# Two-layer decoder trunk on one core: when VectorE forms four sums, splits one small weight, and where seven-product pairs stand in one output product

## The chip, the cores and the metric

The kernel runs on one core of one Trainium2 chip. Its time is the device time in microseconds of the whole program; lower is better. Before the change the median of three runs is 2401.25 us (2401.14, 2401.25 and 2406.06).

## The reference

A trunk of two layers for 256 tokens of width 2048, all in float32. Layer 0 mixes tokens by retention, layer 1 by multi-head latent attention (MLA); each mixer is followed by a SwiGLU. Every sub-layer is `x + post_norm(f(pre_norm(x)))`. What the change touches:

```python
def mla(x, ...):
    c = x @ w_in                                   # latents c_q, c_kv (512 each) and k_r (64)
    c_q, c_kv, k_r = jnp.split(c, [MLA_Q_LORA, MLA_Q_LORA + MLA_KV_LORA], axis=-1)
    ...
    k_rope = rope(k_r[:, :, None, :], positions)   # the rotary key
    ...
    return o @ w_out                               # o: 256 x 2048, w_out: 2048 x 2048

def swiglu(x, w_gu, w_down):                       # in both layers
    gate, up = jnp.split(x @ w_gu, [D_FF], axis=-1)
    return (jax.nn.silu(gate) * up) @ w_down       # D_FF 5632
```

## The kernel before

Each float32 operand is split into a high part (a cast on ScalarE, L210) and a low part (source minus high part, a subtraction on VectorE, L211), and each product is three products on TensorE: high by high, high by low, low by high. SyncE's queue streams the weights as tiles of 128x1024 into four raw buffers; five pairs of slots hold their high and low parts. Matrix products run in the order retention, gu0_0 to gu0_10 (the gate and up product of layer 0, in groups of 1024 columns), dn0 (down), mc (MLA's latents), the rotary key, query products with attention, mlo (MLA's output product, two halves of 1024 columns), gu1_0 to gu1_10, dn1. A group has four PSUM banks: b00 and b01 for the first 128 tokens (t=0), b10 and b11 for the other 128 (t=1), 512 columns each.

Some pairs of weight pieces (two neighbouring tiles of 128 rows) are done as a 2x2 block product with seven products in place of eight. This needs sums of weight blocks and sums of activation blocks, and afterwards sums of the products.

In gu groups 1 to 10 the first four pairs (pieces 0 to 7) are done so, by `first_sevens` (L425). Its tiles are named for what they hold: `b` and `a` are weight blocks and sums t1 to t3, `c` is the second raw tile of a pair, `d` holds t4. TensorE takes the b and a parts of all pairs first, then the c parts on b00 and b01, then the d parts on b10, then pieces 8 to 15 (`w8`, `w9`, ...). `fourth(p)` forms t4 of pair p on VectorE (L473) and splits it at once (`dhi` on ScalarE, `dlo` on VectorE). Between them VectorE also combines banks: L485, L488, L492, L495.

In mlo the function `closing` calls `group` for each half with `sevens` from `MLO_SEVENS`. Pairs of the list take their weight sums (L260 to L263), are split into `ta` and `tb` parts, and run 21 products; behind the last pair of a half, `combine` (L350 to L355) and four `adds` (L360) bring the sums into b00 to b11. In half 0 the pieces behind the last pair are run as they come; in half 1 the t=1 products of the last pieces, and the t=0 products of pieces 14 and 15, are held to the end. The activation sums of a pair are made once, by `left_sums` (L246 to L249), and shared by both halves.

In mc the normed input comes in pieces: TensorE transposes (`htp`, L602), VectorE scales (`hx`, L608), both split it (`hT`). The rotary key's weight `kr_raw` (128x16x64) is split into `kr_w`, used in 16 products (L1100) after mc.

The order on each engine is set by a scheduler from its own costs at build time, unless an instruction goes through `tc.keep_in_program_order`. `later(k, fn)` puts off a call by k weight loads (`step`). On the chip each engine takes its instructions in that fixed order.

Of the kernel before, what the change touches and what calls it, by code (L numbers as in the profile page):

```python
# [8 lines left out]
F32 = mybir.dt.float32  # L9
# [9 lines left out]
DT = D // P  # L19
# [15 lines left out]
GU_SEVENS = 4  # L35
DN_SEVENS = (2, 5, 7, 10, 12, 15, 17), (2, 4, 5, 7, 10, 12, 15, 17)
RTO_SEVENS = (3, 6, 9, 12), (3, 5, 6, 9, 12)
MLO_SEVENS = (3, 5), (1, 3)
QK_SEVENS, VG_SEVENS = (0, 2, 3, 3), 3

C_INV, C_ID, C_MASK, C_TWICE = 0, NF, NF + P, NF + 3 * P
# [17 lines left out]
def trunk(  # L59
# [19 lines left out]
    nc = tc.nc  # L79
# [8 lines left out]
    def misc_bank(name):  # L88
        return ps.tile([P, 512], F32, tag="misc", bufs=2, name=name)
# [43 lines left out]
    def later(k, fn):  # L133
        order[0] += 1
        todo.append((steps[0] + k, order[0], fn))
# [66 lines left out]
    def share(slots, room):  # L202

        both = 2 if slots >= 6 else 1 if slots >= 3 else 0
        return min(2, slots - 2 * both), both, room

    def split(hi, lo, src, g=None):

        if g is None:
            nc.scalar.copy(out=hi, in_=src)  # L210
            nc.vector.tensor_sub(out=lo, in0=src, in1=hi.bitcast(F32))  # L211
        else:
            nc.scalar.activation(out=hi, in_=src, func=AF.Copy, scale=g)
            nc.vector.scalar_tensor_tensor(
                out=lo, in0=src, scalar=g, in1=hi.bitcast(F32), op0=ALU.mult, op1=ALU.subtract
            )

    def weights(load, parts, name, raw_room=None, room=None):


        if raw_room is None:
            raw = wp.tile([P, 1024], F32, tag="raw", bufs=RAW, name=f"{name}_raw")
        else:
            raw = raw_room(F32, f"{name}_xraw")
        load(raw)
        if room is None:
            hi = wp.tile([P, 1024], F32R, tag="whi", bufs=WB, name=f"{name}_hi")
            lo = wp.tile([P, 1024], F32R, tag="wlo", bufs=WB, name=f"{name}_lo")
        else:
            hi, lo = room(F32R, f"{name}_xhi"), room(F32R, f"{name}_xlo")  # L230
        for a, n, g in parts:
            split(hi[:, a : a + n], lo[:, a : a + n], raw[:, a : a + n], g)
        return hi, lo, raw
# [10 lines left out]
    def left_sums(a00, a01, a10, a11, sums, hi, lo):  # L244

        nc.vector.tensor_sub(out=sums[:, 0], in0=a10, in1=a11)  # L246
        nc.vector.tensor_sub(out=sums[:, 1], in0=sums[:, 0], in1=a00)
        nc.vector.tensor_sub(out=sums[:, 2], in0=a00, in1=a10)
        nc.vector.tensor_add(out=sums[:, 3], in0=sums[:, 1], in1=a01)  # L249
        split(hi, lo, sums)  # L250
# [171 lines left out]
                )  # L422
                begun.add(bank)

    def first_sevens(lhs, kts, w, g, name, n, left, spare):  # L425

# [4 lines left out]
        raw1, t2, wt, last = {}, {}, {}, {}  # L433
# [5 lines left out]
        def parts(nm):  # L439
            hi = wp.tile([P, 1024], F32R, tag="whi", bufs=WB, name=f"{name}_{nm}hi")  # L440
            lo = wp.tile([P, 1024], F32R, tag="wlo", bufs=WB, name=f"{name}_{nm}lo")
            return hi, lo

        def half(x, i):
            return tuple(y[:, i * 512 : (i + 1) * 512] for y in x)
# [24 lines left out]
        def fourth(p):  # L470
            if p % 2 == 0:
                last[0] = parts("d")
            nc.vector.tensor_add(out=t2[p], in0=t2[p], in1=raw1[p][:, 0:512])  # L473
            wt["d", p] = half(last[0], p % 2)
            split(*wt["d", p], t2[p])

# [66 lines left out]
    def tile_load(w, g, name, halves=0, spare=(0, 0, None)):  # L543

        def load(kt, first_half=False):
            n = 512 if kt < halves or first_half else 1024  # L550

            def dma(raw):
                for a in range(0, 1024, 512 if kt < halves else 1024):
                    m = 512 if kt < halves else 1024
                    nc.sync.dma_start(out=raw[:, a : a + m], in_=w[g, kt, :, a : a + m])

            parts = [(a, n, None) for a in range(0, 512 if first_half else 1024, n)]
            raws, both, room = spare
            return weights(
                dma, parts, f"{name}_w{kt}", room if DT - 2 - raws <= kt < DT - 2 else None,  # L560
                room if kt >= DT - both else None,
            )

        return load
# [199 lines left out]
    def retention():  # L764
# [34 lines left out]
        def qk_group(gq, spare):  # L799
            name = f"rqk{gq}"  # L800
            if gq:
                return first_sevens(h_lhs, DT, ret_qk, gq, name, QK_SEVENS[gq], lambda p: ins[p], spare)
            return group(h_lhs, DT, tile_load(ret_qk, gq, name, 1, spare), name, lead=3)
# [167 lines left out]
    def swiglu(i):  # L971
        with tc.tile_pool(name=f"ff{i}", bufs=1) as fp:

            groups = FF // 512
            aT = {}

            def spare_a(kind, name):
                return fp.tile([P, 1024], kind, tag="aT", bufs=groups, name=name)

            def take_a(k0, n):  # L980
                return aT[k0 // 4][:, k0 % 4 : k0 % 4 + n]

            def transposes(j, t, a):
                if t == 0:
                    aT[j] = fp.tile([P, 4, NT, P], F32, tag="aT", bufs=groups, name=f"aT{i}{j}")
                tp = misc_bank(f"ftp{i}{j}{t}")
                for b in range(4):
                    nc.tensor.transpose(tp[:, b * P : (b + 1) * P], a[:, b * P : (b + 1) * P], ident)  # L988
                nc.scalar.copy(
                    out=aT[j][:, :, t, :], in_=tp.rearrange("p (j q) -> p j q", j=4)  # L990
                )

            def sums(n):
                f = wp.tile([P, 4, P], F32, tag="mv", bufs=MV, name=f"sf{i}")
                if n < 2:
                    hi = fp.tile([P, 4, P], F32R, tag="sa", bufs=4, name=f"sh{i}")
                    lo = fp.tile([P, 4, P], F32R, tag="sa", bufs=4, name=f"sl{i}")
                else:
                    hi = wp.tile([P, 4, P], F32R, tag="ah", bufs=3, name=f"sh{i}")
                    lo = wp.tile([P, 4, P], F32R, tag="al", bufs=3, name=f"sl{i}")  # L1000
                return f, hi, lo

            ins, where = gu_next[0]
            where[0] = sums

            for j in range(groups):
                name = f"gu{i}_{j}"
                spare = share(groups - j, spare_a)
                if j:
                    banks = first_sevens(  # L1010
                        h_lhs, DT, w_gu[i], j, name, GU_SEVENS, lambda p: ins[p], spare
                    )
                else:
                    banks = group(h_lhs, DT, tile_load(w_gu[i], j, name, 0, spare), name, lead=4)
                watch[0] = None
                both = fp.tile([P, NT, 512], F32, tag="fa", bufs=1, name="fa")
                for t in range(NT):
                    sg = fp.tile([P, 512], F32, tag="fsg", bufs=2, name="fsg")
                    nc.scalar.activation(out=sg, in_=banks[t][0], func=AF.Silu, scale=rx_next[t])
                    a = both[:, t, :]  # L1020
                    nc.vector.scalar_tensor_tensor(
                        out=a, in0=banks[t][1], scalar=rx_next[t], in1=sg, op0=ALU.mult, op1=ALU.mult
                    )
                    later(4 + t, lambda j=j, t=t, a=a: transposes(j, t, a))
            closing(
                take_a, FF // P, w_down[i], g_ffn_post[i],
                None if i else G_MIX + DT, f"dn{i}",
                lambda name: fp.tile([P, 1024], F32, tag="fa", bufs=1, name=name), sevens=DN_SEVENS,
            )


    def mla():
        with tc.tile_pool(name="ml", bufs=1) as mp:
# [18 lines left out]
            with tc.tile_pool(name="ml_c", bufs=1) as cp:  # L1052


                kr_raw = cp.tile([P, DT, ROPE], F32, name="kr_raw")
                kr_w = cp.tile([P, DT, 2, ROPE], F32R, name="kr_w")
                krp = cp.tile([P, 2, NT, P], F32, name="krp")

                def kr_weights():
                    nc.sync.dma_start(out=kr_raw, in_=mla_kr)  # L1060
                    for kt in range(DT):
                        split(
                            kr_w[:, kt, 0, :], kr_w[:, kt, 1, :], kr_raw[:, kt, :]
                        )

                later(10, kr_weights)
                cs = {}

                def kept(banks, t):
# [116 lines left out]
            with tc.tile_pool(name="ml_a", bufs=1) as ap:  # L1186
# [110 lines left out]
                for hp in range(AH // 2):  # L1297
# [5 lines left out]
                    lambda k0, n: oT[:, k0 : k0 + n], AH, mla_out, g_mix_post[1], G_FFN + DT, "mlo",  # L1303
                    lambda name: ap.tile([P, 1024], F32, tag="aqkT", bufs=1, name=name), sevens=MLO_SEVENS,
                )
# [97 lines left out]
```

## Time and profile before

| | |
|---|---|
| median of three runs | 2401.25 us |
| profiled execution | 2400.07 us, span 2398.3 us |
| TensorE (PE) busy | 2382.3 us, 99% of the span |
| VectorE (DVE) busy | 2179.7 us, 91% |
| ScalarE (ACT) busy | 1500.3 us, 63% |
| chain that ended last | PE 94%, DVE 4%, DMA 1%, issue 1%, ACT 1% |
| mean granted TensorE clock | 0.999 |

Matmuls overlap in the pipe: one of 128x512 shows 0.39 us, but a row follows the next in about 0.227 us (787.17 and its neighbours in the trace); "x2" joins neighbours of one kind into one row. Idle time in brackets stands on the engine just before the instruction.

### The profile page before, as it was taken

How to read it: one execution, taken by the hardware profiler on the slowest of the kernel's cores; microseconds unless marked ns; L12 is line 12 of the kernel's file. 1: busy time of each engine (PE TensorE's matmuls, PEld its weight loads, DVE VectorE, ACT ScalarE, POOL GpSimd, SP SyncE). 2: the span in 40 equal slices, each digit the busy share in tenths (PEclk: the TensorE clock that was granted, in tenths of full speed). 3: DMA queues.
4: the chain of work that ended last, by engine and by line, in shares of the span. 5: the costliest groups of instructions: out<-in, count | busy, mean ns of one | idle time of the engine just before them, and what ended most of it. 6: DMA issues, size and time to landing. Idle time of an engine off the chain costs nothing.

```text
span 2398.3 us, 30805 instructions
## 1 busy us (share of the span) xinstructions
PE 2382.3 (99%) x10843; PEld 1971.0 (82%) x10843; DVE 2179.7 (91%) x3112; ACT 1500.3 (63%) x2126; POOL 28.5 (1%) x38
## 2 busy tenths in 40 slices
PE   9999999999999999999999999999999999999998
PEld 7888888888888888888888888887888888888887
DVE  8899888888899999999988987889999999998998
ACT  6555665665666656666666666656666665666664
POOL 0000000000000000000000000000100000000000
PEclk9999999999999999999999999999999999999999
DMA  8555465545656665656456655445666565645655
GB/s 285 187 195 191 167 212 184 170 170 192 206 194 219 207 207 199 209 179 219 161 197 210 200 196 158 129 138 171 234 205 216 177 218 184 212 167 183 221 199 168
DMA packets 129611, 463.76 MB, mean 193 GB/s; under 512 B 14640, under 2 KB 15024, under 8 KB 129456
## 3 DMA queue, kind: packets, MB, share of 16 engines
q1 hardware_dynamic: 129456, 461.80, 57.7%
q8 instruction: 85, 1.39, 0.2%
q14 instruction: 70, 0.57, 0.1%
HBM read 459.64 MB, written 2.10 MB: 193 GB/s over the span
## 4 chain that ended last, share of the span: by engine, by line
PE 94%; DVE 4%; DMA 1%; issue 1%; ACT 1%; SPq 0%; POOL 0%; DVEq 0%; POOLq 0%; ACTq 0%
PE gu_b L419 37%; PE dn_b L419 15%; PE rvg_b L419 14%; PE rqk_b L419 6%; PE rto_b L419 6%; PE q L419 3%; PE dn_m L419 3%; PE mlo_b L419 2%; PE mc_b L419 1%; PE rto_m L419 1%; PE ftp L988 1%; PE ry L916 1%; PE htp L602 0%; PE rsc L861 0%; PE asc L1240 0%
## 5 line engine op out<-in xcount | busy, mean ns | idle before, releaser
L419 PE MATMUL gu_b<-gu_w_hi,hT 128*128 128x512 f32 x1296 | 353.6, 391 | 0.1
L419 PEld LDWEIGHTS gu_b<-gu_w_hi,hT 128*128 128x128 f32 x1296 | 242.3, 188 | 50.6 <-DVE hT L211 0.9
L210 ACT CAST dn_w_hi<-dn_w_raw 128x1024 fp32r<-128x1024 f32 (+1 forms) x176 | 169.1, 978 | 78.4 <-DMA dn_w_raw<-w_down 33.7
L419 PE MATMUL gu_b<-gu_w_lo,hT 128*128 128x512 f32 x648 | 200.4, 391 | 0.0
L211 DVE TENSOR_TENSOR dn_w_lo<-dn_w_raw,dn_w_hi 128x1024 fp32r<-128x1024 f32 (+1 forms) x176 | 193.8, 1130 | 7.1 <-ACT dn_w_hi L210 6.3
L419 PE MATMUL rvg_b<-rvg_w_hi,hT 128*128 128x512 f32 x576 | 157.4, 391 | 0.0
L419 PE MATMUL dn_b<-dn_w_lo,dn_ah 128*128 128x512 f32 x494 | 156.7, 390 | 0.3 <-DVE dn_w_lo L211 0.3
L419 PE MATMUL dn_b<-dn_w_hi,dn_ah 128*128 128x512 f32 x494 | 156.7, 390 | 0.0
L419 PE MATMUL dn_b<-dn_w_hi,dn_al 128*128 128x512 f32 x494 | 156.7, 390 | 0.0
L211 DVE TENSOR_TENSOR gu_w_lo<-gu_w_raw,gu_w_hi 128x1024 fp32r<-128x1024 f32 x122 | 143.6, 1223 | 6.0 <-ACT gu_w_hi L210 6.0
L419 PEld LDWEIGHTS gu_b<-gu_w_lo,hT 128*128 128x128 f32 x648 | 121.2, 188 | 26.3 <-DVE gu_w_lo L211 1.5
L210 ACT CAST gu_w_hi<-gu_w_raw 128x1024 fp32r<-128x1024 f32 x122 | 122.5, 1049 | 29.2 <-PE gu_b L419 11.3
L419 PEld LDWEIGHTS rvg_b<-rvg_w_hi,hT 128*128 128x128 f32 x576 | 107.7, 188 | 22.0
L210 ACT CAST gu_ahi<-gu_ta 128x1024 fp32r<-128x1024 f32 x80 | 84.4, 1055 | 46.7 <-PE gu_b L419 36.0
L211 DVE TENSOR_TENSOR gu_clo<-gu_s,gu_chi 128x1024 fp32r<-128x1024 f32 x80 | 97.6, 1222 | 14.7 <-ACT gu_chi L210 13.4
L419 PEld LDWEIGHTS dn_b<-dn_w_lo,dn_ah 128*128 128x128 f32 x494 | 92.7, 188 | 19.8 <-DVE dn_w_lo L211 0.7
L419 PEld LDWEIGHTS dn_b<-dn_w_hi,dn_ah 128*128 128x128 f32 x494 | 92.8, 188 | 19.2
L419 PEld LDWEIGHTS dn_b<-dn_w_hi,dn_al 128*128 128x128 f32 x494 | 92.8, 188 | 19.2
L211 DVE TENSOR_TENSOR gu_alo<-gu_ta,gu_ahi 128x1024 fp32r<-128x1024 f32 x80 | 97.8, 1223 | 7.0 <-ACT gu_ahi L210 6.9
L210 ACT CAST gu_bhi<-gu_s 128x512 fp32r<-128x512 f32 x80 | 49.7, 622 | 81.6 <-PE gu_b L419 65.9
L419 PE MATMUL rqk_b<-rqk_w_hi,hT 128*128 128x512 f32 x352 | 99.4, 396 | 1.2 <-ACT rqk_w_hi L210 1.1
L210 ACT CAST gu_chi<-gu_s 128x1024 fp32r<-128x1024 f32 x80 | 83.8, 1051 | 13.6 <-PE gu_b L419 13.4
(535 smaller groups left out, 6284.9 us busy)
## 6 DMA issues: line engine op xcount, KB each, us to landing
dn_w_raw<-w_down SPq DMA_DIRECT2D x176, 512.0 KB, 4.5
gu_s<-w_gu SPq DMA_DIRECT2D x160, 512.0 KB, 4.6
gu_w_raw<-w_gu SPq DMA_DIRECT2D x152, 512.0 KB, 3.7
rvg_w_raw<-ret_vg SPq DMA_DIRECT2D x67, 512.0 KB, 4.4
rto_w_raw<-ret_out SPq DMA_DIRECT2D x64, 512.0 KB, 4.3
rvg_s<-ret_vg SPq DMA_DIRECT2D x48, 512.0 KB, 4.2
rqk_w_raw<-ret_qk SPq DMA_DIRECT2D x43, 512.0 KB, 4.3
gu_w_xraw<-w_gu SPq DMA_DIRECT2D x40, 512.0 KB, 5.2
```

The lines of the kernel that those rows point to most:

```text
L210: nc.scalar.copy(out=hi, in_=src)
L211: nc.vector.tensor_sub(out=lo, in0=src, in1=hi.bitcast(F32))
L419: nc.tensor.matmul(out, e[2](), e[3](), start=bank not in begun, stop=ends[bank, added.get(bank, 0)] == n, skip_group_check=bank in added,)
L916: nc.tensor.matmul(y, left, right, start=n == 0, stop=n == len(terms) - 1)
L988: nc.tensor.transpose(tp[:, b * P : (b + 1) * P], a[:, b * P : (b + 1) * P], ident)
```

## The change

Four places. `split` and `first_sevens` take an optional `pin`. For group 1 of both SwiGLUs (gu0_1 and gu1_1: two of the four places) the t4 sums of L473 are kept in program order. The rotary key's weight is split in one cast and one subtraction of 128x16x64, both kept in program order, in place of sixteen of 128x64 each; its DMA is due two loads earlier, its split three loads later. In mlo, half 1 takes pairs 3 and 5 as seven products in place of 1 and 3, so that activation sums are made for two pairs in place of three. The number of products on TensorE is unchanged.

```diff
--- before.py
+++ after.py
@@ -35,7 +35,7 @@
 GU_SEVENS = 4
 DN_SEVENS = (2, 5, 7, 10, 12, 15, 17), (2, 4, 5, 7, 10, 12, 15, 17)
 RTO_SEVENS = (3, 6, 9, 12), (3, 5, 6, 9, 12)
-MLO_SEVENS = (3, 5), (1, 3)
+MLO_SEVENS = (3, 5), (3, 5)
 QK_SEVENS, VG_SEVENS = (0, 2, 3, 3), 3
 
 C_INV, C_ID, C_MASK, C_TWICE = 0, NF, NF + P, NF + 3 * P
@@ -204,11 +204,11 @@
         both = 2 if slots >= 6 else 1 if slots >= 3 else 0
         return min(2, slots - 2 * both), both, room
 
-    def split(hi, lo, src, g=None):
+    def split(hi, lo, src, g=None, pin=lambda ins: ins):
 
         if g is None:
-            nc.scalar.copy(out=hi, in_=src)
-            nc.vector.tensor_sub(out=lo, in0=src, in1=hi.bitcast(F32))
+            pin(nc.scalar.copy(out=hi, in_=src))
+            pin(nc.vector.tensor_sub(out=lo, in0=src, in1=hi.bitcast(F32)))
         else:
             nc.scalar.activation(out=hi, in_=src, func=AF.Copy, scale=g)
             nc.vector.scalar_tensor_tensor(
@@ -422,7 +422,7 @@
                 )
                 begun.add(bank)
 
-    def first_sevens(lhs, kts, w, g, name, n, left, spare):
+    def first_sevens(lhs, kts, w, g, name, n, left, spare, pin=lambda ins: ins):
 
 
 
@@ -470,7 +470,7 @@
         def fourth(p):
             if p % 2 == 0:
                 last[0] = parts("d")
-            nc.vector.tensor_add(out=t2[p], in0=t2[p], in1=raw1[p][:, 0:512])
+            pin(nc.vector.tensor_add(out=t2[p], in0=t2[p], in1=raw1[p][:, 0:512]))
             wt["d", p] = half(last[0], p % 2)
             split(*wt["d", p], t2[p])
 
@@ -1008,7 +1008,8 @@
                 spare = share(groups - j, spare_a)
                 if j:
                     banks = first_sevens(
-                        h_lhs, DT, w_gu[i], j, name, GU_SEVENS, lambda p: ins[p], spare
+                        h_lhs, DT, w_gu[i], j, name, GU_SEVENS, lambda p: ins[p], spare,
+                        *((tc.keep_in_program_order,) if j == 1 else ()),
                     )
                 else:
                     banks = group(h_lhs, DT, tile_load(w_gu[i], j, name, 0, spare), name, lead=4)
@@ -1057,13 +1058,10 @@
                 krp = cp.tile([P, 2, NT, P], F32, name="krp")
 
                 def kr_weights():
-                    nc.sync.dma_start(out=kr_raw, in_=mla_kr)
-                    for kt in range(DT):
-                        split(
-                            kr_w[:, kt, 0, :], kr_w[:, kt, 1, :], kr_raw[:, kt, :]
-                        )
-
-                later(10, kr_weights)
+                    split(kr_w[:, :, 0, :], kr_w[:, :, 1, :], kr_raw, pin=tc.keep_in_program_order)
+
+                later(8, lambda: nc.sync.dma_start(out=kr_raw, in_=mla_kr))
+                later(13, kr_weights)
                 cs = {}
 
                 def kept(banks, t):
```

The first place is VectorE in gu0_1, from the t4 sums to the d parts (`t2` is t4's tile, `mv` and `bNN` the combining of banks). Before:

```order
L473 TENSOR_TENSOR gu0_1_t2_7116<-gu0_1_t2_7116,gu0_1_s1_7113 128x512
L473 TENSOR_TENSOR gu0_1_t2_7160<-gu0_1_t2_7160,gu0_1_s1_7157 128x512
L473 TENSOR_TENSOR gu0_1_t2_7191<-gu0_1_t2_7191,gu0_1_s1_7188 128x512
L211 TENSOR_TENSOR gu0_1_clo_7229<-gu0_1_s1_7085,gu0_1_chi_7228 128x1024
L485 TENSOR_TENSOR gu0_1_mv1_7213<-gu0_1_b01_7080,gu0_1_mv0_7208 128x512
L211 TENSOR_TENSOR gu0_1_clo_7236<-gu0_1_s1_7113,gu0_1_chi_7235 128x1024
L488 TENSOR_TENSOR gu0_1_b10_7081<-gu0_1_b10_7081,gu0_1_mv1_7213 128x512
L492 TENSOR_TENSOR gu0_1_b01_7080<-gu0_1_b11_7082,gu0_1_mv1_7213 128x512
L211 TENSOR_TENSOR gu0_1_clo_7243<-gu0_1_s1_7157,gu0_1_chi_7242 128x1024
L495 TENSOR_TENSOR gu0_1_b11_7082<-gu0_1_b11_7082,gu0_1_mv0_7208 128x512
L211 TENSOR_TENSOR gu0_1_clo_7250<-gu0_1_s1_7188,gu0_1_chi_7249 128x1024
L211 TENSOR_TENSOR gu0_1_dlo_7269<-gu0_1_t2_7088,gu0_1_dhi_7268 128x512
```

After:

```order
L211 TENSOR_TENSOR gu0_1_clo_7250<-gu0_1_s1_7188,gu0_1_chi_7249 128x1024
L495 TENSOR_TENSOR gu0_1_b11_7082<-gu0_1_b11_7082,gu0_1_mv0_7208 128x512
L473 TENSOR_TENSOR gu0_1_t2_7088<-gu0_1_t2_7088,gu0_1_s1_7085 128x512
L211 TENSOR_TENSOR gu0_1_dlo_7269<-gu0_1_t2_7088,gu0_1_dhi_7268 128x512
L473 TENSOR_TENSOR gu0_1_t2_7116<-gu0_1_t2_7116,gu0_1_s1_7113 128x512
L211 TENSOR_TENSOR gu0_1_dlo_7269<-gu0_1_t2_7116,gu0_1_dhi_7268 128x512
L473 TENSOR_TENSOR gu0_1_t2_7160<-gu0_1_t2_7160,gu0_1_s1_7157 128x512
L211 TENSOR_TENSOR gu0_1_dlo_7283<-gu0_1_t2_7160,gu0_1_dhi_7282 128x512
L473 TENSOR_TENSOR gu0_1_t2_7191<-gu0_1_t2_7191,gu0_1_s1_7188 128x512
L211 TENSOR_TENSOR gu0_1_w8_lo_7299<-gu0_1_w8_raw_7296,gu0_1_w8_hi_7298 128x1024
L211 TENSOR_TENSOR gu0_1_w9_lo_7317<-gu0_1_w9_raw_7314,gu0_1_w9_hi_7316 128x1024
L211 TENSOR_TENSOR gu0_1_dlo_7283<-gu0_1_t2_7191,gu0_1_dhi_7282 128x512
```

The three later sums of L473 stood together ahead of the first `clo`; now each of the four stands behind `clo` and L495, with the `dlo` of the pair before it between them, and the fourth `dlo` stands behind two weight pieces. On TensorE the c parts of three pairs now come first on b00, and w8 stands ahead of the last d products; gu1_1 changes alike.

The second place is ScalarE in mc, where the split of the rotary key's weight stood among the casts of the normed input. Before:

```order
L210 CAST hT_12821<-hx10_12932 128x2x128
L210 CAST kr_w_12873<-kr_raw_12872 128x64 x6
L210 CAST hT_12821<-hx11_12940 128x2x128
L210 CAST kr_w_12873<-kr_raw_12872 128x64 x2
L127 ACTIVATE junk_62,dn0_nx1_10762<-xs_72 128x512
L210 CAST mc_w5_hi_13024<-mc_w5_raw_13022 128x1024
```

After:

```order
L210 CAST hT_12821<-hx10_12932 128x2x128
L210 CAST hT_12821<-hx11_12940 128x2x128
L127 ACTIVATE junk_62,dn0_nx1_10762<-xs_72 128x512
L210 CAST mc_w5_hi_13024<-mc_w5_raw_13022 128x1024
L127 ACTIVATE junk_62,dn0_nx0_10761<-xs_72 128x512
L210 CAST mc_w6_hi_13053<-mc_w6_raw_13051 128x1024
```

The eight small casts of this stretch are gone, as are the eight that stood further down; the one large cast now stands behind the cast of mc_w12.

The third place is VectorE in half 1 of mlo, where the seven products are combined (`m` are their banks). Before, behind pair 3 as the last pair:

```order
L211 TENSOR_TENSOR mlo1_w3_tblo_15416<-mlo1_w3_tb_15406,mlo1_w3_tbhi_15415 128x1024
L211 TENSOR_TENSOR mlo1_w8_lo_15458<-mlo1_w8_raw_15455,mlo1_w8_hi_15457 128x1024
L351 TENSOR_TENSOR mlo1_mv1_15441<-mlo1_m6_15325,mlo1_mv0_15440 128x512
L211 TENSOR_TENSOR mlo1_w9_lo_15470<-mlo1_w9_raw_15467,mlo1_w9_hi_15469 128x1024
L352 TENSOR_TENSOR mlo1_mv2_15442<-mlo1_m7_15327,mlo1_mv1_15441 128x512
L211 TENSOR_TENSOR mlo_al_15494<-oT_12864,mlo_ah_15493 128x512
L353 TENSOR_TENSOR mlo1_mv1_15441<-mlo1_m5_15326,mlo1_mv1_15441 128x512
L355 TENSOR_TENSOR mlo1_mx_15447<-mlo1_m5_15326,mlo1_mv2_15442 128x512
L360 TENSOR_TENSOR mlo1_b00_15242<-mlo1_b00_15242,mlo1_mv0_15440 128x512
L360 TENSOR_TENSOR mlo1_b01_15243<-mlo1_b01_15243,mlo1_mv1_15441 128x512
```

After, behind pair 5:

```order
L211 TENSOR_TENSOR mlo1_w12_lo_15500<-mlo1_w12_raw_15497,mlo1_w12_hi_15499 128x1024
L351 TENSOR_TENSOR mlo1_mv1_15485<-mlo1_m6_15367,mlo1_mv0_15484 128x512
L211 TENSOR_TENSOR mlo1_w13_lo_15512<-mlo1_w13_raw_15509,mlo1_w13_hi_15511 128x1024
L352 TENSOR_TENSOR mlo1_mv2_15486<-mlo1_m7_15369,mlo1_mv1_15485 128x512
L211 TENSOR_TENSOR mlo1_w14_lo_15526<-mlo1_w14_raw_15523,mlo1_w14_hi_15525 128x1024
L353 TENSOR_TENSOR mlo1_mv1_15485<-mlo1_m5_15368,mlo1_mv1_15485 128x512
L355 TENSOR_TENSOR mlo1_mx_15491<-mlo1_m5_15368,mlo1_mv2_15486 128x512
L211 TENSOR_TENSOR mlo1_w15_lo_15532<-mlo1_w15_raw_15529,mlo1_w15_hi_15531 128x1024
L360 TENSOR_TENSOR mlo1_b00_15212<-mlo1_b00_15212,mlo1_mv0_15484 128x512
L360 TENSOR_TENSOR mlo1_b01_15213<-mlo1_b01_15213,mlo1_mv1_15485 128x512
L360 TENSOR_TENSOR mlo1_b10_15214<-mlo1_b10_15214,mlo1_mv2_15486 128x512
L360 TENSOR_TENSOR mlo1_b11_15215<-mlo1_b11_15215,mlo1_mx_15491 128x512
```

The combining is the same; ahead of the adds there are now w12 to w15 in place of w8 and w9, and the last operation ahead of them is a split of 1024 columns where it was a sum of 512.

## Rows read from the trace of the kernel before

**Rows 1.** Part 1 of the page: busy time of each engine, share of the span, instructions.

```profile
PE 2382.3 (99%) x10843; PEld 1971.0 (82%) x10843; DVE 2179.7 (91%) x3112; ACT 1500.3 (63%) x2126; POOL 28.5 (1%) x38
```

**Rows 2.** The waits of TensorE over the span: us in total, times, longest us.

```profile
PE mc_b L419 <- ACT hT L210: 1.1, 2, 0.7
```

**Rows 3.** Timeline of TensorE in gu0_1: start, duration, instruction, [idle before <-releaser].

```profile
787.17 0.63 PE L419 MATMUL gu_b<-gu_chi,hT 128*128 128x512 f32 x2
788.49 0.50 PE L419 MATMUL gu_b<-gu_clo,hT 128*128 128x512 f32 x1 [0.69 <-DVE gu_clo L211]
...
789.70 0.50 PE L419 MATMUL gu_b<-gu_chi,sh 128*128 128x512 f32 x1 [0.23 <-DVE gu_b L492]
...
795.29 0.39 PE L419 MATMUL gu_b<-gu_dlo,hT 128*128 128x512 f32 x1
```

**Rows 4.** Timeline of VectorE in gu0_1.

```profile
783.67 1.90 DVE L473 TENSOR_TENSOR gu_t<-gu_t,gu_s 128x512 f32<-128x512 f32 x3
785.47 1.23 DVE L211 TENSOR_TENSOR gu_clo<-gu_s,gu_chi 128x1024 fp32r<-128x1024 f32 x1
786.61 0.69 DVE L485 TENSOR_TENSOR gu_mv<-gu_b,gu_mv 128x512 f32<-128x512 f32 x1
...
792.40 2.50 DVE L211 TENSOR_TENSOR gu_dlo<-gu_t,gu_dhi 128x512 fp32r<-128x512 f32 x4
```

**Rows 5.** Timeline of ScalarE in gu0_1.

```profile
783.95 2.00 ACT L210 CAST gu_chi<-gu_s 128x1024 fp32r<-128x1024 f32 x2
...
788.21 1.14 ACT L210 CAST gu_dhi<-gu_t 128x512 fp32r<-128x512 f32 x2
```

**Rows 6.** Timeline of ScalarE and VectorE, one hand-over between them in gu1_2.

```profile
1787.57 0.62 ACT L210 CAST gu_bhi<-gu_s 128x512 fp32r<-128x512 f32 x1 [0.98 <-PE gu_b L419]
...
1788.22 0.69 DVE L211 TENSOR_TENSOR gu_blo<-gu_s,gu_bhi 128x512 fp32r<-128x512 f32 x1 [0.28 <-ACT gu_bhi L210]
```

**Rows 7.** Timeline of ScalarE and TensorE in gu1_1.

```profile
1749.71 1.99 ACT L210 CAST gu_chi<-gu_s 128x1024 fp32r<-128x1024 f32 x2
...
1755.45 0.50 PE L419 MATMUL gu_b<-gu_chi,sh 128*128 128x512 f32 x1
...
1761.03 0.39 PE L419 MATMUL gu_b<-gu_dlo,hT 128*128 128x512 f32 x1
```

**Rows 8.** Timeline of ScalarE, VectorE and TensorE in mc.

```profile
1428.29 1.03 ACT L210 CAST mc_w_hi<-mc_w_raw 128x1024 fp32r<-128x1024 f32 x1
...
1433.83 0.98 ACT L210 CAST kr_w<-kr_raw 128x64 fp32r<-128x64 f32 x6 [1.56 <-DMA kr_raw<-mla_kr]
...
1435.15 0.42 DVE L211 TENSOR_TENSOR hT<-hx,hT 128x256 fp32r<-128x256 f32 x1 [0.86 <-ACT hT L210]
1435.50 1.22 DVE L211 TENSOR_TENSOR mc_w_lo<-mc_w_raw,mc_w_hi 128x1024 fp32r<-128x1024 f32 x1
...
1440.70 0.69 DVE L608 TENSOR_TENSOR hx<-htp,gcol 128x512 f32<-128x512 f32 x1
...
1440.97 0.71 PE L419 MATMUL mc_b<-mc_w_hi,hT 128*128 128x512 f32 x2
1442.36 0.73 PE L419 MATMUL mc_b<-mc_w_hi,hT 128*128 128x512 f32 x2 [0.67 <-ACT hT L210]
```

**Rows 9.** Timeline of TensorE in half 1 of mlo.

```profile
1656.00 0.39 PE L419 MATMUL mlo_b<-mlo_w_hi,mlo_s 128*128 128x512 f32 x1
...
1658.14 0.50 PE L419 MATMUL mlo_m<-mlo_w_tbhi,mlo_s 128*128 128x512 f32 x1 [1.06 <-ACT mlo_w_tbhi L210]
```

**Rows 10.** Timeline of TensorE and VectorE in half 0 of mlo, pair 5.

```profile
1633.11 0.39 PE L419 MATMUL mlo_m<-mlo_w_hi,mlo_ah 128*128 128x512 f32 x1
...
1640.92 1.29 DVE L360 TENSOR_TENSOR mlo_b<-mlo_b,mlo_mv 128x512 f32<-128x512 f32 x2
```

**Rows 11.** Windows: from:to, length, busy us (x instructions) of PE, PEld, DVE, ACT, POOL; PEclk, DMA share, GB/s.

```profile
0.00:5.00 5.00, 3.38 (x8) 1.12 (x9) 0.29 (x2) 1.28 (x1) 0.20 (x4) 1.00 0.57 132
...
10.00:20.00 10.00, 10.00 (x45) 8.11 (x45) 9.33 (x20) 9.40 (x19) 0.00 (x0) 0.86 0.92 327
```

## The prediction

> **What bounds the kernel now.** I read part 1 of the page first: TensorE is busy for 2382.3 of 2398.3 us [rows 1], so 16.0 us of idle time is all that a better order could give back over the whole program. Next come TensorE's waits: the reader is to see that they are few and short, as the two of 1.1 us together on the normed input in mc [rows 2]. Last I read the timelines at the places that the change reorders, and ask at each what TensorE is due to take, when VectorE or ScalarE has it ready, and what stands ahead of it on that engine. A change that only reorders can gain at most the waits it removes, and loses wherever it puts a longer chain in front of TensorE.
>
> The measures are read from starts. A matmul follows the last in 0.227 us; the first one behind a wait shows 0.50 in place of 0.39 [rows 3], so I charge 0.1 more for each restart. On VectorE an operation of 128x512 lets the next start after 0.60 us, one of 128x1024 after 1.14 (three sums from 783.67 to 785.47, one split from 785.47 to 786.61) and lasts 0.69 and 1.23 [rows 4]. A ScalarE cast of 128x512 lasts 0.62, and VectorE takes its result 0.03 later [rows 6]; I take 0.03 in the other direction too. Two casts of 128x1024 take 2.00, so the first is done after 1.05 and a further one costs 0.95 [rows 5].
>
> **The t4 sums in gu0_1 and gu1_1.** Before, three sums ran at 783.67 and all four `dlo` at 792.40 in one go, since their casts had begun at 788.21 [rows 4, 5]. After, each sum stands behind the `dlo` of the pair before it, and each `dlo` waits for a cast that waits for its own sum. One turn of this chain is sum 0.69 + 0.03 + cast 0.62 + 0.03 + 0.60 until VectorE goes on behind `dlo` = 1.97 us. TensorE's three products of a pair take 3 x 0.227 = 0.68. So TensorE, not VectorE, waits: 1.29 us in each turn.
>
> In gu0_1 the first `clo` can start when its cast is done: 783.95 + 1.05 + 0.03 = 785.03 [rows 5]. Then VectorE has four `clo` (4 x 1.14) and four bank operations (4 x 0.60) before the first sum: 785.03 + 6.96 = 791.99. The first `dlo` starts 0.69 + 0.03 + 0.62 + 0.03 = 1.37 later, at 793.36; the third two turns later, at 797.30, and is done 0.69 on: 797.99. TensorE took the low product of the third pair at 795.29 [rows 3] and can take it now at 798.02: +2.73, and 0.1 for the restart. The fourth cast stands behind two weight casts: the third is done at 797.27, two more at 0.95 each, then 0.62 gives about 799.75. TensorE has one product and three of w8 to fill in, until 798.02 + 0.34 + 4 x 0.227 = 799.27, and waits 0.5 and 0.1. Sum: +3.4 us. This holds the wait that was there before: 29 products lie between 787.17 and 795.29, 6.6 us of work in 8.1, which is the 1.5 us lost on `clo` and L492 [rows 3]. It moves; it doesn't come on top.
>
> In gu1_1 the same count from the cast at 1749.71 [rows 7]: first `clo` 1750.79, first sum 1757.75, third `dlo` done at 1763.75, the product at 1763.78 in place of 1761.03: +2.75, again +0.1 and about +0.55 for the fourth. Sum: +3.4 us. Before, only 0.2 us was lost here, around 1755.45, so the loss is new.
>
> Bounds for the two together: if the fourth pair costs nothing, 2 x 2.8 = 5.6; if each restart and hand-over costs twice what I charge (five per group more at about 0.1), 7.8. I take 6.8. The weight splits that VectorE does later (w8_lo near 798.5) meet a TensorE that is late by the same 3.4 us; without that cover each further late split would cost up to 1.14.
>
> **The rotary key's weight in mc.** Six small casts waited 1.56 us for their DMA, until 1433.83, with the normed input's cast behind them; VectorE waited 0.86 us for that cast, and stayed late until it scaled the next piece at 1440.70 [rows 8]. TensorE, due at 1440.97 + 2 x 0.227 = 1441.42, got this piece at 1442.36: 0.94 and 0.1 for the restart. In the changed order these small casts are gone from there, VectorE is some 0.9 us earlier, the piece's cast done by 1441.1 or so: -1.0 us. What is late next is nothing that the waits show [rows 2]. Bounds: -1.05; 0 if VectorE at 1440.70 was held by its weight splits alone. Sixteen casts and sixteen subtractions become one each; both engines have this time free, so that part is costed at nothing. The one cast now stands ahead of a later piece of the normed input; TensorE's held products of earlier pieces cover it, and if they didn't it would cost a cast of its size, 1.05. The DMA moved earlier is one transfer on SyncE's queue, between the same two weight loads as before: nothing.
>
> The Trainium skill, "Perfetto Trace Analysis", Optimizing Scalar/DVE Operations, advises breaking up instructions on engines that aren't saturated but cause bubbles elsewhere, which speaks against the merged cast. By it the gain here would be lost again to the later piece, and the sum would be 1.0 higher; the rows show the small casts themselves holding the queue, so I do not take it.
>
> **Half 1 of mlo.** Pair 1's sums came late: from 1656.00 to 1658.14 there are three steps of 0.227 and 1.46 us of wait, 1.57 with the restart [rows 9]. With pairs 3 and 5 this wait goes: half 0 runs the same pairs, and pair 5 begins there without one [rows 10]. A new one comes behind pair 5. In half 0 its products began at 1633.11 and the first add came at 1640.92, 7.81 us later [rows 10]. In half 1 the operation ahead of the adds is the split of w15, 1.14 in place of a 128x512 split's 0.60, so the add starts at 8.35 and is done at 9.04. TensorE has 21 products of the pair and 12 of pieces 12 and 13 on the first banks, 33 x 0.227 = 7.49 us, and then needs b00: it waits 1.6 and 0.1. Before, it had pieces 8 and 9 for both token halves, 12 products more, and needed no wait. Net +0.1 us; bounds -1.57 if the adds come in time, +1.1 if w15's cast is a further 1.0 late. Two left-over terms, one fewer activation sum (four operations of 128x128 and a split of 512 on VectorE) and a few weight loads in another order at gu1_0, lie under TensorE's work: nothing, within 0.8 either way.
>
> **Sum.** +3.4 + 3.4 - 1.0 + 0.1 = +5.9 us on the profiled execution's 2400.07, so 2406.0. The median shown, 2401.25, is 1.2 above that execution: 2407.1. A change of 0.2% (4.8 us) is about what a measurement of this kernel tells from none; the forecast is just beyond it, on the slower side.
>
> **Rivals.** *Not slower, the chain hidden.* If the first sum began by 791.99 - 2.73 = 789.26, the d parts would be ready as before and everything else would gain: -1.5 - 0.2 - 1.0 + 0.1 = -2.6, 2398.7; without the new wait in mlo -4.3, 2397.0, still within 0.2%. For it: the sums' inputs are there early, they ran at 783.67 [rows 4]. It needs VectorE to run a sum 2.7 us ahead of its place in the queue. Against: the weight split at 1435.50 had had its cast since 1428.29 + 1.03, and stood until the split ahead of it, which waited 0.86 us, had gone [rows 8]. The Trainium skill, "PSUM — Partial Sum Buffer", Engine vs sequencer instructions, says that ScalarE's and VectorE's queues are strictly first in, first out; by that rule the hidden chain is out, and the trace agrees. I give it 0.09.
>
> *Half the price.* If the chain overlaps in part (the casts' place on ScalarE, the c parts earlier), gu costs 1.7 in each layer: +2.5, 2403.8. For it: VectorE no longer runs three sums ahead of `clo`. Against: I have counted that already, and ScalarE had idle time here. 0.16.
>
> *The clock.* At the start TensorE was busy 3.38 of 5 us, and the granted clock of the stretch from 10 to 20 was 0.86 though it was busy throughout, a mixture of 1.2 and 2.4 GHz [rows 11]; that costs 1.4 us. In the gu groups it would be busy for some 70% of 15 us too. If each costs 1.4: +2.8, 2409.9. Against: each wait here is about 1.3 us and products go on between. The skill's "TensorE: Matmul & The Clock Gate", Part 1, ties the lower level to an engine that is idle; by that rule an engine that goes on taking products between its waits loses nothing. 0.11.
>
> *No effect*, orders that cost what the old ones did: 2401.25, 0.04.
>
> **Chances and range.** The forecast has 0.60, with its own range 2405 to 2409.5. Slower by over 0.2%: most of the forecast (0.51) and the clock (0.11), 0.62. Faster by over 0.2%: would need more than all waits at these places, 0.03. Within: 0.35. The range from 2400.5 to 2410.5 takes in half the price and the clock and leaves the hidden chain out.
>
> **What would show it.** In gu0_1 and gu1_1 TensorE should wait for `dhi` (L210) and `dlo` (L211) by turns, some 0.7 and 0.4 us, two or three times each, and VectorE should show sum and `dlo` alternating at 1.97 us a pair. The `clo` wait of 0.69 may stay. In mc the wait of 0.67 on `hT` should be gone and the rotary key's cast be one instruction. In mlo the wait on `tbhi` should be gone and one of about 1.6 us on L360 stand behind pair 5. The forecast is wrong if the four `dlo` of a group come in one go, or if TensorE waits less than 3 us in all over either gu stretch.

## The result and the profile after

The changed kernel takes 2408.98 us (median of 11 runs, 2407.22 to 2410.88), the kernel before 2402.85 in the same series (11 runs): a ratio of 1.0029, 95% interval 1.0021 to 1.0037, so slower by 5 to 9 us. The forecast was +5.9 us, 2407.1 in all; of the 1.9 us that it falls short, 1.6 are in the kernel before, whose median rose from the 2401.25 that the forecast started from. The profiled execution's span is 2405.6 us, 7.3 more than before.

Part 1 of the page of the changed kernel answers to [rows 1]:

```profile
PE 2386.2 (99%) x10843; PEld 1969.1 (82%) x10843; DVE 2179.1 (91%) x3092; ACT 1498.9 (62%) x2110; POOL 25.6 (1%) x38
```

VectorE and ScalarE are as busy as before. TensorE's idle time grew from 16.0 to 19.4 us, and its busy time by 3.9 at the same number of products: a part of each wait stands in the rows as busy, since the ends of products are modelled. So a loss is better read from starts than from the idle time in brackets. TensorE's waits in the changed kernel, to be read against [rows 2] (us in total, times, longest):

```profile
PE gu_b L419 <- ACT gu_dhi L210: 2.7, 6, 0.6
PE mlo_b L419 <- DVE mlo_b L360: 1.5, 1, 1.5
...
PE gu_b L419 <- ACT fsg L1020: 1.1, 1, 1.1
PE gu_b L419 <- DVE gu_dlo L211: 0.9, 4, 0.2
...
PE mc_b L419 <- ACT hT L210: 0.4, 1, 0.4
PE gu_b L419 <- DVE gu_clo L211: 0.3, 1, 0.3
```

The first and the fourth line are new: ten waits on the d parts, in the two pinned groups alone. The second is new too and is the add in mlo. `fsg` is the tile of the SiLU (L1019 before, L1020 here), which empties a bank of the group before; its wait, 0.4 us before, is at the start of gu1_1. One of the two waits in mc is gone, as is the one on `tbhi` in mlo [rows 9].

TensorE in gu0_1 of the changed kernel, start first; it answers to [rows 3]:

```profile
788.83 0.50 PE L419 MATMUL gu_b<-gu_clo,hT 128*128 128x512 f32 x1 [0.35 <-DVE gu_clo L211]
...
790.04 0.50 PE L419 MATMUL gu_b<-gu_chi,sh 128*128 128x512 f32 x1 [0.24 <-DVE gu_b L492]
...
795.05 0.50 PE L419 MATMUL gu_b<-gu_dhi,hT 128*128 128x512 f32 x1 [0.52 <-ACT gu_dhi L210]
795.77 0.50 PE L419 MATMUL gu_b<-gu_dlo,hT 128*128 128x512 f32 x1 [0.23 <-DVE gu_dlo L211]
...
797.08 0.50 PE L419 MATMUL gu_b<-gu_dhi,hT 128*128 128x512 f32 x1 [0.57 <-ACT gu_dhi L210]
797.81 0.50 PE L419 MATMUL gu_b<-gu_dlo,hT 128*128 128x512 f32 x1 [0.23 <-DVE gu_dlo L211]
...
799.50 0.50 PE L419 MATMUL gu_b<-gu_dhi,hT 128*128 128x512 f32 x1 [0.26 <-ACT gu_dhi L210]
```

The reader is to see the turns: dhi, dlo, dhi, dlo, 0.5 and 0.2 us, each with a slow restart (0.50 for the product). The brackets understate the loss: between the first and the last of the group's twelve products on the d parts they add up to 1.9 us, while the starts, at 0.227 us for each product, lie 3.6 us too far apart. It is 3.6 in gu1_1 too, and 0.0 in both groups of the kernel before. VectorE in the same stretch, against [rows 4]:

```profile
791.63 0.68 DVE L473 TENSOR_TENSOR gu_t<-gu_t,gu_s 128x512 f32<-128x512 f32 x1
793.05 0.69 DVE L211 TENSOR_TENSOR gu_dlo<-gu_t,gu_dhi 128x512 fp32r<-128x512 f32 x1 [0.74 <-ACT gu_dhi L210]
793.66 0.68 DVE L473 TENSOR_TENSOR gu_t<-gu_t,gu_s 128x512 f32<-128x512 f32 x1
795.03 0.69 DVE L211 TENSOR_TENSOR gu_dlo<-gu_t,gu_dhi 128x512 fp32r<-128x512 f32 x1 [0.68 <-ACT gu_dhi L210]
795.64 0.69 DVE L473 TENSOR_TENSOR gu_t<-gu_t,gu_s 128x512 f32<-128x512 f32 x1
797.06 0.69 DVE L211 TENSOR_TENSOR gu_dlo<-gu_t,gu_dhi 128x512 fp32r<-128x512 f32 x1 [0.74 <-ACT gu_dhi L210]
```

Sum and `dlo` by turns, 1.98 and 2.03 us a pair where 1.97 was worked out, and VectorE itself sits idle for 0.7 us in each turn. ScalarE's part, against [rows 5]:

```profile
792.40 0.62 ACT L210 CAST gu_dhi<-gu_t 128x512 fp32r<-128x512 f32 x1 [2.33 <-DVE gu_t L473]
794.38 0.62 ACT L210 CAST gu_dhi<-gu_t 128x512 fp32r<-128x512 f32 x1 [1.36 <-DVE gu_t L473]
796.41 0.62 ACT L210 CAST gu_dhi<-gu_t 128x512 fp32r<-128x512 f32 x1 [1.42 <-DVE gu_t L473]
```

Before, the casts took 1.14 us for two in one go; now each waits for its own sum.

What a group costs is read from the same place in it, the transposes of the group before (`ftp`, L988). In the kernel before, those that stand in gu0_1 and in gu0_2, then in gu1_1 and in gu1_2:

```profile
779.71 1.03 PE L988 MATMUL ftp<-cst,fa 128*128 128x128 f32 x8
...
822.95 1.03 PE L988 MATMUL ftp<-cst,fa 128*128 128x128 f32 x8
...
1746.75 1.03 PE L988 MATMUL ftp<-cst,fa 128*128 128x128 f32 x8
...
1788.69 1.04 PE L988 MATMUL ftp<-cst,fa 128*128 128x128 f32 x8
```

In the changed kernel:

```profile
779.73 1.03 PE L988 MATMUL ftp<-cst,fa 128*128 128x128 f32 x8
...
826.16 1.04 PE L988 MATMUL ftp<-cst,fa 128*128 128x128 f32 x8
...
1750.06 1.03 PE L988 MATMUL ftp<-cst,fa 128*128 128x128 f32 x8
...
1795.56 1.03 PE L988 MATMUL ftp<-cst,fa 128*128 128x128 f32 x8
```

43.24 us became 46.43 in layer 0 (+3.2), 41.94 became 45.50 in layer 1 (+3.6). Layer 0 shows less because gu0_1 before had waits of its own, as long as they happened to be in that execution: in the four other kernels with the old order there it takes 42.57 to 42.94. By the starts of the first product of each stage, mc became 0.8 us shorter, mlo stayed (0.0), and gu1_0 with the start of gu1_1 became 1.2 longer.

### The profile page after: what moved, and what is told of

It is laid out like the page before. It is cut to its first block, busy times and chain, and to the rows that moved or that the text cites. A ratio compares the mean times of both kernels' runs of the same rounds, so it can differ in the third digit from the quotient of the medians.

```text
span 2405.6 us, 30776 instructions
## 1 busy us (share of the span) xinstructions
PE 2386.2 (99%) x10843; PEld 1969.1 (82%) x10843; DVE 2179.1 (91%) x3092; ACT 1498.9 (62%) x2110; POOL 25.6 (1%) x38
## 4 chain that ended last, share of the span: by engine, by line
PE 91%; DVE 5%; ACT 1%; issue 1%; DMA 1%; SPq 0%; POOL 0%; DVEq 0%; POOLq 0%; ACTq 0%
PE gu_b L419 33%; PE dn_b L419 16%; PE rvg_b L419 14%; PE rqk_b L419 6%; PE rto_b L419 6%; PE dn_m L419 3%; PE q L419 3%; PE mlo_b L419 3%; PE mc_b L419 2%; PE rto_m L419 1%; DVE gu_w_lo L211 1%; PE ftp L988 1%; PE ry L916 1%; DMA gu_s<-w_gu 1%; PE asc L1238 0%
## 5 line engine op out<-in xcount | busy, mean ns | idle before, releaser
L419 PEld LDWEIGHTS dn_b<-dn_w_hi,dn_ah 128*128 128x128 f32 x494 | 92.7, 188 | 19.4 <-DVE dn_y L732 0.2
L419 PEld LDWEIGHTS dn_b<-dn_w_hi,dn_al 128*128 128x128 f32 x494 | 92.7, 188 | 19.4
```

The source lines that it names most:

```text
L419: nc.tensor.matmul(out, e[2](), e[3](), start=bank not in begun, stop=ends[bank, added.get(bank, 0)] == n, skip_group_check=bank in added,)
```

## The experiments

Intervals are against the kernel before, which ran again beside the experiments: its median is 2401.44 us beside 1, 2, 3 and 5, and 2400.58 beside 4, 6 and 7. Kernels of different series are compared by their ratios. A single span is not compared: dn0, where no instruction differs, was from 0.8 us shorter to 2.3 longer than before in these profiled executions. Stretches are.

**1. Without the pin.** Changed kernel, minus one line:

```diff
-                        *((tc.keep_in_program_order,) if j == 1 else ()),
```

> The changed kernel without the pin on the t4 sums; the rotary key's split and the pairs of mlo stay as changed. Theory (the pin's chain of sum, cast, dlo is the loss): the waits on gu_dhi and gu_dlo are gone in both layers, gu0_1 again loses some 1.5 us on clo and L492, and the time is 6.7 us below the changed kernel's, some 0.5 us from the kernel before (-0.9 in mc, 0 in mlo, +1.1 in gu1_0). Rival (the loss comes from the later pairs in mlo, which leave VectorE late for layer 1): gu1_1 keeps at least half of its 3.5 us, and the time is 2 to 4 us above the kernel before.

Measured: 2400.05 us, ratio 0.9996 (0.9987 to 1.0005), by the ratios 0.33% below the changed kernel, some 7.9 us, where 6.7 was told. Its waits:

```profile
PE mlo_b L419 <- DVE mlo_b L360: 1.5, 1, 1.5
...
PE gu_b L419 <- ACT fsg L1019: 0.7, 1, 0.7
PE mc_b L419 <- ACT hT L210: 0.4, 1, 0.4
PE gu_b L419 <- DVE gu_b L492: 0.2, 1, 0.2
```

The d parts are gone from the list, and gu1_1 is as long as before (+0.0). This speaks for the pin and against mlo as the source. One expectation missed: the wait on `clo` in gu0_1 is gone as well, though VectorE's order there is that of the kernel before. VectorE was 0.6 us earlier against TensorE in this execution; so of the 1.5 us that I read as lost there [rows 3], 0.7 was that execution's chance.

**2. The pin alone.** Kernel before, with only the lines of the change in `first_sevens` and its call:

```diff
-            nc.vector.tensor_add(out=t2[p], in0=t2[p], in1=raw1[p][:, 0:512])
+            pin(nc.vector.tensor_add(out=t2[p], in0=t2[p], in1=raw1[p][:, 0:512]))
...
+                        *((tc.keep_in_program_order,) if j == 1 else ()),
```

> The kernel before with the pin on the t4 sums alone. Theory: +3.2 us in gu0_1 and +3.5 us in gu1_1, +6.7 us in all against the kernel before, VectorE with sum and dlo by turns at 1.98 us a pair. Rival (gu1_1 is late because of mlo): +3.2 in gu0_1 and under 2 in gu1_1, +5 or less.

Measured: 2408.61 us (6 runs), ratio 1.0031 (1.0019 to 1.0042). The pin alone gives the whole loss: from transposes to transposes +3.6 us in gu0_1 and +4.5 in gu1_1. That is more than the chain: in each of the two groups TensorE's granted clock fell to its lower level for a while, which costs 0.9 to 1.1 us (the rows are under the rivals below).

```profile
PE gu_b L419 <- ACT gu_dhi L210: 2.2, 4, 0.6
...
PE mlo_m L419 <- ACT mlo_w_tbhi L210: 1.1, 1, 1.1
PE gu_b L419 <- DVE gu_dlo L211: 0.9, 4, 0.2
```

**3. The four sums together.** Changed kernel; the sums keep their place behind L495 (`together` is a new argument, true where the pin is given):

```diff
-            pin(nc.vector.tensor_add(out=t2[p], in0=t2[p], in1=raw1[p][:, 0:512]))
+            for q in (range(n) if p == 0 else ()) if together else (p,):
+                pin(nc.vector.tensor_add(out=t2[q], in0=t2[q], in1=raw1[q][:, 0:512]))
```

> The changed kernel with the four pinned sums of a group issued together, ahead of the four splits, in gu0_1 and gu1_1; the first sum stays behind L495. Theory (what costs is the hand-over from VectorE to ScalarE and back in each pair): one wait of about 1.2 us on the first dlo of each group stays, then the products run through; +0.9 us in gu0_1 and +1.2 in gu1_1 against the kernel before, so 4.6 us below the changed kernel. Rival (what costs is that the sums stand behind L495 at all): the group ends no more than 1 us earlier than in the changed kernel, which is 2 us or less in all.

Measured: 2402.75 us, ratio 1.0007 (0.9998 to 1.0016), some 5 us below the changed kernel; gu0_1 is 2.5 us shorter than there and gu1_1 2.2, where 2.3 each was worked out. Of ten waits on the d parts two are left:

```profile
PE gu_b L419 <- DVE gu_dlo L211: 2.0, 2, 1.0
```

Against experiment 1 the pinned groups lose 7.4 us, and 4.6 of them come back: two thirds of the loss is the passing back and forth in each pair, one third that the sums come late, with the first `dlo` now behind all four. The two thirds include the fourth pair, whose cast stands here behind one weight cast in place of two. Neither theory alone has all of it, though the first told the size.

**4. The pin in two groups.** Changed kernel:

```diff
-                        *((tc.keep_in_program_order,) if j == 1 else ()),
+                        *((tc.keep_in_program_order,) if j in (1, 2) else ()),
```

> The changed kernel with the pin on the t4 sums in groups 1 and 2 of both layers, so four groups in place of two. Theory (each pinned group costs its own chain of three turns): gu0_2 and gu1_2 each become 3.2 to 3.9 us longer, with the same waits on gu_dhi and gu_dlo; 6.5 to 8 us above the changed kernel, 0.55 to 0.65% above the kernel before. Rival (the first group behind a norm costs so much because VectorE comes to it late; a later group hides the chain): the added groups cost under 1.5 us each, and the time is 3 us or less above the changed kernel.

Measured: 2416.52 us (5 runs), ratio 1.0065 (1.0053 to 1.0078), by the ratios 8.6 us above the changed kernel, where 6.5 to 8 was expected. gu0_2 and gu1_2 each became 3.5 us longer, and the ten waits became eighteen:

```profile
PE gu_b L419 <- ACT gu_dhi L210: 4.9, 10, 0.6
PE gu_b L419 <- DVE gu_dlo L211: 1.8, 8, 0.2
```

A later group hides nothing; the chain's price is its own. What was not expected is group 1, pinned as in the changed kernel: gu0_1 is 1.5 us longer than there and gu1_1 1.0, since the granted clock fell in both, as in experiment 2, and the wait on `clo` in gu0_1 is 0.7 in place of 0.35. In gu0_2 and gu1_2 it did not fall.

**5. The pairs of mlo alone.** Kernel before:

```diff
-MLO_SEVENS = (3, 5), (1, 3)
+MLO_SEVENS = (3, 5), (3, 5)
```

> The kernel before with pairs 3 and 5 in half 1 of mlo, and nothing else. Theory (the new order in mlo costs what it saves and leaves VectorE and the DMA of gu1_1's first tiles late): the wait on tbhi of 1.06 us is gone, one of 1.5 us on L360 is there, and the wait on fsg at the start of gu1_1 is 1.1 us in place of 0.4; +1.1 us against the kernel before. Rival (the later start in gu1_1 was a slow transfer in that one execution): fsg waits 0.4 us as before, and the time is within 0.3 us of the kernel before.

Measured: 2400.54 us, ratio 0.9999 (0.9990 to 1.0009): the time tells neither from the other.

```profile
PE mlo_b L419 <- DVE mlo_b L360: 1.5, 1, 1.5
...
PE gu_b L419 <- ACT fsg L1019: 0.7, 1, 0.7
```

In place of `tbhi` stands the add, and mlo is as long as before (0.0). Then gu1_0 is 0.5 us longer; so it is in all five kernels with these pairs (0.5 to 0.6), and in none of the three others (-0.2 to 0.0). The wait on `fsg` is 0.7 here, 1.1 in the changed kernel, but also 1.0 in the kernel of experiment 6, which has the old pairs: that part is not due to mlo, and what sets it is left open. So the theory holds for the add and for the 0.5, and not for `fsg`.

**6. The rotary key's split alone.** Kernel before with the change's lines in `kr_weights`:

```diff
-                    nc.sync.dma_start(out=kr_raw, in_=mla_kr)
-                    for kt in range(DT):
-                        split(
-                            kr_w[:, kt, 0, :], kr_w[:, kt, 1, :], kr_raw[:, kt, :]
-                        )
-
-                later(10, kr_weights)
+                    split(kr_w[:, :, 0, :], kr_w[:, :, 1, :], kr_raw, pin=tc.keep_in_program_order)
+
+                later(8, lambda: nc.sync.dma_start(out=kr_raw, in_=mla_kr))
+                later(13, kr_weights)
```

> The kernel before with the rotary key's split alone changed. Theory (the small casts held up the normed input's casts in mc): of the two waits on hT in mc the second, 0.67 us, is gone and the first, 0.4, stays; some 0.9 us below the kernel before between the start of mc and the rotary key's products, and nothing elsewhere. Rival (the casts were in ScalarE's idle time and cost nothing): both waits stay, within 0.2 us in that stretch. In the whole time both are under what can be told; the trace decides.

Measured: 2399.48 us, ratio 0.9996 (0.9987 to 1.0005). From the start of mc to the rotary key's products it is 0.8 us shorter, as in every kernel with this split (0.8 to 0.9), and longer by 0.2 to 0.4 in the two without. One wait on `hT` is left where [rows 2] had two, beside the `fsg` of experiment 5:

```profile
PE gu_b L419 <- ACT fsg L1019: 1.0, 1, 1.0
...
PE mc_b L419 <- ACT hT L210: 0.4, 1, 0.4
```

**7. Pairs 2 and 4 in mlo.** Changed kernel without the pin:

```diff
-MLO_SEVENS = (3, 5), (3, 5)
+MLO_SEVENS = (2, 4), (2, 4)
```

> The changed kernel without the pin and with pairs 2 and 4 in both halves of mlo, in place of 3 and 5. Theory (the add waits because TensorE has only 12 products between the last pair and its next use of b00): behind pair 4 it has 24, so the wait of 1.5 us on L360 is gone; VectorE isn't left late and the wait on fsg falls to 0.4 us or less. 1.5 to 2.2 us below the same kernel with pairs 3 and 5, 2 to 3 us below the kernel before. Rival (VectorE is too late in half 1 whichever pairs are taken): a wait of 1 us or more on tbhi or on L360 comes back, and the time is within 0.5 us of the same kernel with pairs 3 and 5.

Measured: 2399.35 us, ratio 0.9994 (0.9985 to 1.0003). mlo is 2.0 us shorter than with pairs 3 and 5, no wait on mlo is left in the list, and `fsg` is short:

```profile
PE mc_b L419 <- ACT hT L210: 0.4, 1, 0.4
PE gu_b L419 <- ACT fsg L1019: 0.3, 1, 0.3
```

The wait on the add came from what TensorE has to do between the last pair and its next use of b00: from the pair's first product to the first add there are still 7.8 us, against 8.3 with pairs 3 and 5, but TensorE has 12 products (2.7 us) more to take meanwhile. In the whole time the expectation is not confirmed: by the ratios it is 1.4 us below the kernel before, where 2 to 3 was told, and 0.5 below experiment 1, where 1.5 to 2.2 was, and neither difference is clear of its interval. It is the lowest median here and clearly below the changed kernel, but not shown to beat the kernel before.

## Why the prediction held

**The chain in the pinned groups** was the step that decided, and it held in its place, its form and its size: +3.4 us per group was worked out, +3.2 and +3.6 were measured, with experiments 1, 2 and 4 for the cause and 3 for the mechanism. Part of the fit in gu0_1 is luck: the 1.5 us that the chain was to take over from the old waits were 0.7 too many, and against the other kernels with the old order the group lost 3.5 to 3.9. Single waits came out shorter in the brackets: on `dhi` 0.5 to 0.6 where 0.7 was told, on `dlo` 0.2 where 0.4 was; the 0.1 of a restart makes up most of the difference. The prediction also called itself wrong if TensorE waited less than 3 us in all over either gu stretch. By the brackets that sign came true (1.9 us on the d parts in each group); by the starts, in which the loss had been worked out, it did not (3.6 us). It should have said which of the two it meant. The first sum came at 791.63, not 791.99, since ScalarE was 0.3 us early.

**mc**: -1.0 told, -0.8 measured. **mlo**: +0.1 told, 0.0 measured. The adds in the changed kernel, VectorE first:

```profile
1677.87 0.69 DVE L211 TENSOR_TENSOR mlo_al<-oT,mlo_ah 128x512 fp32r<-128x512 f32 x1
...
1684.63 1.22 DVE L211 TENSOR_TENSOR mlo_w_lo<-mlo_w_raw,mlo_w_hi 128x1024 fp32r<-128x1024 f32 x1
1685.76 1.89 DVE L360 TENSOR_TENSOR mlo_b<-mlo_b,mlo_mv 128x512 f32<-128x512 f32 x3
```

and TensorE:

```profile
1677.47 0.39 PE L419 MATMUL mlo_m<-mlo_w_hi,mlo_ah 128*128 128x512 f32 x1
...
1686.60 0.47 PE L419 MATMUL mlo_b<-mlo_w_hi,mlo_ah 128*128 128x512 f32 x1 [1.49 <-DVE mlo_b L360]
```

From the pair's first product to the first add there are 8.29 us, where 8.35 was told, and TensorE waits 1.49, where 1.6 was. The split of w15 ends where the add starts, so VectorE's order sets it; how long the add would wait for the last products on b00 alone was not tried.

**What was missed** is gu1_0: "nothing, within 0.8 either way" is +0.5 us from the new pairs and +0.6 from `fsg`. Together that is 1.1, outside what was allowed. With this the stretches come to some +7.1; the rest of the span's +7.3 lies in stages without a changed instruction. The medians differ by 6.1, so close to the forecast's 5.9 by luck: the interval is 5 to 9 us, and the sum lacked these 1.1. The 0.5 belongs in the sum for mlo, since it comes and goes with the pairs; that its order leaves VectorE later at the start of gu1_0 is the likely reason, and was not tried.

**The rivals.** The hidden chain fell: VectorE took the sums where the order has them. Half the price fell with the +3.2 and +3.6 above and the +3.5 of experiment 4. The clock did not fall in the profiled execution of the changed kernel, by the row of the pinned stretch (length, then busy us of PE, PEld, DVE, ACT, POOL, then the granted clock):

```profile
783.00:801.00 18.00, 15.54 (x61) 10.51 (x60) 15.18 (x20) 11.36 (x16) 0.00 (x0) 1.00 0.53 182
```

TensorE is busy for 15.54 of 18 us and the granted clock is 1.00, the higher of its two levels, unlike in [rows 11]. But the rival is not gone. In experiments 2 and 4 the clock did fall in group 1 of both layers, at about the third pair's low product. A stretch of gu0_1 in each, first experiment 2, then experiment 4:

```profile
797.00:799.00 2.00, 2.00 (x6) 1.52 (x6) 2.00 (x3) 2.00 (x4) 0.00 (x0) 0.50 0.78 256
```

```profile
800.00:802.00 2.00, 2.00 (x7) 1.57 (x6) 2.00 (x4) 1.88 (x2) 0.00 (x0) 0.50 0.89 238
```

0.50 is the lower level, 1.2 GHz. From the third pair's product on `dlo` to the next transposes there are 28.35 us in the changed kernel, in both layers, and 29.28 to 29.44 in these four groups: 0.9 to 1.1 us for each fall, where the rival had told 1.4. What TensorE did just before does not tell the two apart, first experiment 2, then the changed kernel at the same place of the chain:

```profile
792.00:796.00 4.00, 2.63 (x7) 0.97 (x6) 2.58 (x5) 1.79 (x3) 0.00 (x0) 1.00 0.82 246
```

```profile
793.60:797.60 4.00, 2.60 (x7) 0.97 (x6) 2.58 (x5) 1.80 (x3) 0.00 (x0) 1.00 0.74 247
```

The instructions are the same and the busy time is too; the clock fell in one and not in the other. In the kernels without the chain, and in experiment 3, it stayed at 1.00 in all these groups. So the rule on which the prediction leaned against this rival, that an engine which goes on taking products between its waits loses nothing, does not hold in these runs: the longest wait in the chain shows 0.6 us, and the clock fell. Whether the clock also fell in other executions of the changed kernel, and so has a part in its 6.1 us, is not shown.

## What to carry to other kernels

Where a value goes from one engine to a second and back, issue all that the first engine can do before the first hand-over; interleaving operation and result pair by pair turns a queue into a chain, and here the chain takes 2 us for 0.7 us of products. A chain of short waits can cost more than its waits, if the clock falls in it. Before trusting a written order, follow one turn of it through all the engines, with durations of the trace. A wait in the timeline of one execution may be that execution's own, so a gain that consists of removing it may not be there.

## What was not expected of the hardware

TensorE and VectorE drift against each other between executions of the same instructions: the wait of 0.69 us on `clo` in gu0_1 [rows 3] was absent in experiments 1 and 5, 0.3 in 6, 0.4 in 7. And dn0, the same in all of these kernels, spread over 3 us. The granted clock differs in the same way: with the same instructions and the same busy time it fell to 0.50 in the pinned group 1 of experiments 2 and 4 and stayed at 1.00 in that of the changed kernel; what decides it is open.
